# The entry of a one-core decoder kernel: token block on ScalarE's queue, weights first on SyncE's, eight warm-up products from a narrower tile of zeros

## The chip, the cores and the metric

The kernel runs on one core of a Trainium2 chip. Its time is the device's time of one execution in microseconds. The engines are TensorE (PE; its weight loads are listed as PEld), VectorE (DVE), ScalarE (ACT), GpSimd (POOL) and SyncE (SP). SP and ACT issue DMAs on a queue each; "SPq" and "ACTq" in the trace are these issues.

## The reference, cut to what matters

Two transformer layers on 256 tokens of width 1024 in float32. Only the first steps are touched by the change:

```
def reference(x, norm_gain, sb_w_qkv, ...):
    h = x
    for layer in range(DEPTH):                       # DEPTH = 2
        hn = rms_norm(h, norm_gain[layer, 0])
        if layer < N_A_LAYERS:                       # layer 0
            h = h + stick_breaking_attention(hn, sb_w_qkv[layer], sb_w_o[layer])
        else:                                        # layer 1
            h = h + nsa_attention(hn, nsa_w_q[j], nsa_gate_b[j], nsa_w_o[j], shared)
        h = h + sqrelu_mlp(rms_norm(h, norm_gain[layer, 1]), mlp_w1[layer], mlp_w2[layer])
        if layer == N_A_LAYERS - 1:
            shared = nsa_shared_kv(h, kv_norm, nsa_w_kv, cmp_pos, cmp_w1, cmp_w2)
    return rms_norm(h, final_norm)

def stick_breaking_attention(h, w_qkv, w_o):
    qkv = (h @ w_qkv).reshape(b, s, 3, SB_HEADS, HEAD_DIM)
    ...
```

The first product that the kernel computes is the V part of `h @ w_qkv`.

## The kernel before, in words

Every float32 matrix product is done as three products of "float32r" parts: each operand is split into a high part (a cast, on ACT) and a low part (operand less high part, on DVE). For weights the tiles are `raw` (as loaded), `wh` (high, line 180) and `wl` (low, line 186); for tokens the pair `xa` is made from `xin` (the transposed tokens, as loaded) times the norm's gains `gc`. `mm3` issues the three products at lines 261 (high by high), 262 (high tokens by low weights) and 263 (low tokens by high weights).

Layer 0 begins in `layer0`. In the order of the source:

- Nine warm-up products into the bank `warm` (`mm`, line 266). Both operands are `zero`, a tile of 128 x 512 bfloat16 zeros which DVE fills at line 289. Nothing reads their result.
- Buffers for four weight tiles `raw` are taken with `fetch()`. The gains are loaded on ACT's queue (line 672). Then SP's queue gets, in this order: the first of eight token blocks (`x_load(0, 1)`, line 656, 128 x 256 floats, 128 KB), two quarters of the first weight tile (`v_load`, line 124, 256 KB each), the second token block, two more quarters, and so on; behind them constants, the identity and the untransposed tokens (lines 688 to 693).
- `x_cut` makes the high and low parts of a token block: for block 0 the high part on DVE (line 663), for the others on ACT (line 665); the low part always on DVE (line 666).
- `v_proj(k)` for k = 0 to 7 multiplies token block k with its weights: two halves of 512 columns, in each two halves of tokens, in each the three products, into four banks `pv`. So a token block has 12 products, in two groups of six.

ACT begins with loading its table of functions (line 63). In layer 0 the order of PE's work is a planner's, from the order of the source; in much of the rest it is kept as written (`strict`, `keep_in_program_order`). Later weight tiles go through a ring of `raw` buffers, loaded on SP's queue as buffers come free.

Of the kernel before, what the change touches and what calls it, by code (L numbers as in the profile page):

```python
# [9 lines left out]
BF16 = mybir.dt.bfloat16  # L10
# [4 lines left out]
P = 128  # L15
# [37 lines left out]
def hybrid_kernel(ctx, tc, x, xca, xcb, eye, gcols, gfin, wqk, wva, wvb, wo0, wkv, wq, wg, rot, wo1, w1, w2, cw1, cw2, cpos, gate_b, cmask, consts, out):  # L53
    nc = tc.nc

    cp = ctx.enter_context(tc.tile_pool(name="cp", bufs=1))
# [11 lines left out]
    def big(shape, dt, name):  # L68
        return cp.tile(shape, dt, tag="e", name=name, bufs=3)
# [8 lines left out]
    def bank2(name):  # L78
        return ps.tile([P, 512], F32, tag="z", name=name, bufs=4)
# [17 lines left out]
    def fetch():  # L97

        while ahead[0] < len(stream) and stream[ahead[0]][2]:
            ahead[0] += 1  # L100
        if ahead[0] < len(stream):
            j = ahead[0]
            src, n, _ = stream[j]
            if more:
                more[1] += 1
                if more[1] % 5 == 0 and j > more[2]:
                    more.clear()
                    return
            if more and more[1] % 5 == 0:
                raws[j] = more[0]  # L110
            elif j == NV - 1:
                raws[j] = big([P, n], F32, "raw")
            else:
                raws[j] = wp.tile([P, n], F32, tag="raw", name="raw", bufs=4)
            if j in mixed:
                nc.sync.dma_start(raws[j][:, 0:1536], src[:, 512:2048])
            elif j >= NV:
                nc.sync.dma_start(raws[j], src)
            ahead[0] += 1

    def v_load(j, a, b):
        q = 2 * j + a // D
        src = wva[4 * j + a // 512] if q < 3 else wvb[q - 3]
        nc.sync.dma_start(raws[j][:, a:b], src)
# [131 lines left out]
    def pe(ins):  # L256
        if strict[0]:
            tc.keep_in_program_order(ins)
# [6 lines left out]
    def mm(o, a, b, first, last):  # L265
        pe(nc.tensor.matmul(o, a, b, start=first, stop=last, skip_group_check=True))  # L266
# [18 lines left out]
    def cut(hl, a, b):  # L285
        return hl[0][:, a:b], hl[1][:, a:b]

    zero = cp.tile([P, 512], BF16, name="zero")
    nc.vector.memset(zero, 0.0)
    ident = cp.tile([P, P], F32, name="ident")  # L290
    hres = [cp.tile([P, D], F32, name=f"hres{t}") for t in range(T)]
# [46 lines left out]
    def xt_tiles(tag):  # L338
        xp = cp.tile([P, NK, 2, T * P], F32R, tag="x", name=f"x{tag}", bufs=2)
        return xp[:, :, 0, :], xp[:, :, 1, :], xp  # L340
# [292 lines left out]
    def layer0(ap):  # L633

        warm = bank2("warm")
        for i in range(9):
            mm(warm, zero[:, 0:P], zero, True, True)
        xt = xt_tiles("a")
        v = big([P, T, D], F32, "v0")
        pv = [[bank(f"pv{t}{n}") for n in range(2)] for t in range(T)]  # L640
# [11 lines left out]

        xin = big([P, NK, T * P], F32, "xin")

        def x_load(k, m):
            nc.sync.dma_start(xin[:, k:k + m, :].rearrange("p k q -> p (k q)"), xca[k] if m == 1 else xcb)

        def x_cut(k, m):

# [9 lines left out]

        for j in range(NV):  # L670
            fetch()
        nc.scalar.dma_start(gc, gcols)
        x_load(0, 1)
        v_load(0, 0, 512)
        v_load(0, 512, D)
        x_load(1, 1)
        v_load(0, D, D + 512)
        v_load(0, D + 512, 2 * D)
        x_load(2, 1)
        v_load(1, 0, 512)  # L680
        v_load(1, 512, D)
# [520 lines left out]
    def scoped(f, name, *a, bufs=2):  # L1202
        with tc.tile_pool(name=name, bufs=bufs) as ap:
            return f(*a, ap)

    xn = scoped(layer0, "l0")
    nxt = []

# [190 lines left out]
```

## Time and profile before

| | |
|---|---|
| time, median of 3 runs | 600.16 us (599.56 to 601.12) |
| profiled execution, device time | 600.3 us |
| its span, first to last instruction | 598.4 us |
| busy share of the span | PE 98%, PEld 83%, DVE 88%, ACT 70%, POOL 17% |
| granted clock, mean | 0.996 |
| first warm-up product / first product of real data | 1.19 us / 4.65 us |

A row of the timeline reads: start in us, duration in us, engine, line, operation, output <- inputs, shapes, count; in brackets, how long the engine was idle before it and what released it. A row of the waits reads: who waited <- for what: total us, times, longest. In the windows by engine each engine has its busy time and, in brackets, how many instructions; then come the granted clock, the DMA engines' busy share and GB/s. A DMA row has the size of one issue in KB and the median time from issue to landing in us. The ends of products are modelled: a product's row is longer than the distance to the next one.

### The profile page before, as it was taken

How to read it: one execution, taken by the hardware profiler on the slowest of the kernel's cores; microseconds unless marked ns; L12 is line 12 of the kernel's file. 1: busy time of each engine (PE TensorE's matmuls, PEld its weight loads, DVE VectorE, ACT ScalarE, POOL GpSimd, SP SyncE). 2: the span in 40 equal slices, each digit the busy share in tenths (PEclk: the TensorE clock that was granted, in tenths of full speed). 3: DMA queues.
4: the chain of work that ended last, by engine and by line, in shares of the span. 5: the costliest groups of instructions: out<-in, count | busy, mean ns of one | idle time of the engine just before them, and what ended most of it. 6: DMA issues, size and time to landing. Idle time of an engine off the chain costs nothing.

```text
span 598.4 us, 9128 instructions
## 1 busy us (share of the span) xinstructions
PE 587.8 (98%) x3407; PEld 494.0 (83%) x3407; DVE 527.3 (88%) x809; ACT 419.5 (70%) x663; POOL 103.4 (17%) x132
## 2 busy tenths in 40 slices
PE   9999999999999999999999999999999999999994
PEld 6888887888888888888998778678888888888884
DVE  5598997889999999999786898855899999999995
ACT  6677774787777777784841697854887677778753
POOL 0201130020211121000222255460101121111001
PEclk9999999999999999999999999999999999999998
DMA  8977356676999899954477732447678898999501
GB/s 313 423 291 247 141 153 165 245 186 222 264 236 268 271 263 272 287 210 150 156 263 281 251 139 72 142 115 158 173 223 272 214 281 267 246 308 260 175 0 72
DMA packets 27069, 129.81 MB, mean 217 GB/s; under 512 B 3344, under 2 KB 4624, under 8 KB 18320
## 3 DMA queue, kind: packets, MB, share of 16 engines
q1 hardware_dynamic: 19392, 104.18, 47.9%
q0 software_dynamic: 6624, 24.12, 20.4%
q10 hardware_dynamic: 1008, 0.92, 0.5%
q8 instruction: 27, 0.44, 0.3%
q14 instruction: 18, 0.15, 0.1%
HBM read 127.11 MB, written 1.05 MB: 214 GB/s over the span
## 4 chain that ended last, share of the span: by engine, by line
PE 92%; DVE 4%; ACT 2%; issue 1%; POOLq 0%; POOL 0%; DVEq 0%; ACTq 0%
PE pu L266 29%; PE acc L261 8%; PE qk L266 7%; PE acc L262 7%; PE acc L263 7%; PE po L266 3%; PE pu L261 3%; PE pu L262 3%; PE pu L263 3%; PE z L266 2%; PE pk L261 2%; PE pk L262 2%; PE pk L263 2%; PE ptp L269 2%; PE pv L261 1%; PE pv L262 1%
## 5 line engine op out<-in xcount | busy, mean ns | idle before, releaser
L180 ACT CAST wh<-raw 128x1024 fp32r<-128x1024 f32 (+1 forms) x126 | 126.1, 1022 | 35.1 <-PE pq L262 7.7
L266 PE MATMUL pu<-xn,wh 128*128 128x512 f32 x512 | 131.4, 391 | 0.0
L186 DVE TENSOR_TENSOR wl<-raw,wh 128x1024 fp32r<-128x1024 f32 (+1 forms) x90 | 107.1, 1208 | 26.4 <-ACT wh L180 24.5
L266 PEld LDWEIGHTS pu<-xn,wh 128*128 128x128 f32 x512 | 95.3, 188 | 19.4
L266 PE MATMUL pu<-xn,wl 128*128 128x256 f32 x512 | 76.5, 282 | 0.0
L266 PEld LDWEIGHTS pu<-xn,wl 128*128 128x128 f32 x512 | 72.1, 190 | 5.1
L449 ACT COPY mr<-pu 128x512 f32<-128x512 f32 x64 | 37.3, 582 | 36.5 <-PE pu L266 36.1
L388 POOL DMA_DIRECT2D tx<-in_w x26 | 23.0, 930 | 171.4 <-DMA tx<-in_w 170.9
L477 ACT CAST hh<-hx 128x896 fp32r<-128x896 f32 (+1 forms) x32 | 29.6, 925 | 16.7 <-DVE hx L467 11.7
L512 DVE TENSOR_TENSOR wl<-raw,wh 128x2048 fp32r<-128x2048 f32 x18 | 41.1, 2285 | 0.0
L261 PE MATMUL acc<-wh,hh 128*128 128x512 f32 x96 | 37.8, 394 | 0.1
L262 PE MATMUL acc<-wl,hh 128*128 128x512 f32 x96 | 37.6, 392 | 0.0
L136 DVE TENSOR_TENSOR wl<-raw,wh 128x1536 fp32r<-128x1536 f32 x21 | 36.8, 1751 | 0.6 <-ACT wh L135 0.6
L263 PE MATMUL acc<-wh,hl 128*128 128x512 f32 x96 | 37.0, 390 | 0.0
L135 ACT CAST wh<-raw 128x1536 fp32r<-128x1536 f32 x21 | 31.1, 1483 | 5.5 <-PE pu L266 4.7
L387 POOL DMA_DIRECT2D tx<-in_w x20 | 18.7, 936 | 94.2 <-DVE xn L335 57.5
L478 DVE TENSOR_TENSOR hl<-hx,hh 128x896 fp32r<-128x896 f32 (+1 forms) x32 | 34.1, 1066 | 0.3 <-ACT hh L477 0.3
L136 DVE TENSOR_TENSOR tp<-tx,tp 128x1024 fp32r<-128x1024 f32 x28 | 34.1, 1218 | 0.3
L1127 POOL TENSOR_TENSOR pe<-pe,rs 128x512 f32<-128x512 f32 (+1 forms) x32 | 29.3, 946 | 27.0 <-DVE rs L1122 9.9
L266 PE MATMUL qk<-xa,wh 128*128 128x512 f32 x128 | 32.5, 394 | 0.0
L135 ACT CAST tp<-tx 128x1024 fp32r<-128x1024 f32 x28 | 29.5, 1053 | 3.6 <-DVE tx L203 3.5
L1113 ACT ACTIVATE pe<-pe,nm 128x256 f32<-128x256 f32 (+1 forms) x64 | 28.2, 442 | 4.1 <-DVE nm L1111 3.1
(258 smaller groups left out, 1415.0 us busy)
## 6 DMA issues: line engine op xcount, KB each, us to landing
raw<-in_w SPq DMA_DIRECT2D x31, 1024.0 KB, 6.7
tx<-in_w POOLq DMA_DIRECT2D x46, 512.0 KB, 8.6
raw<-in_w SPq DMA_DIRECT2D x21, 768.0 KB, 6.4
raw<-in_wqk SPq DMA_DIRECT2D x8, 1024.0 KB, 8.1
raw<-in_wo SPq DMA_DIRECT2D x8, 1024.0 KB, 4.8
tx<-in_w SPq DMA_DIRECT2D x7, 1024.0 KB, 5.6
raw<-in_wkv SPq DMA_DIRECT2D x6, 1024.0 KB, 4.7
raw<-in_wq SPq DMA_DIRECT2D x4, 1024.0 KB, 4.9
```

The costliest lines, as they stand in the source:

```text
L135: act(nc.scalar.copy(dh[:, r], src[:, r]))
L136: return lambda: dve(nc.vector.tensor_sub(dl[:, r], src[:, r], f32(dh[:, r])))
L180: ins = nc.scalar.copy(h[:, r], raws[j][:, r])
L186: dve(nc.vector.tensor_sub(lo[:, r], raws[j][:, r], f32(h[:, r])))
L261: pe(nc.tensor.matmul(o, a[0], b[0], start=first, stop=False, skip_group_check=True))
L262: pe(nc.tensor.matmul(o, a[0], b[1], start=False, stop=False, skip_group_check=True))
L263: pe(nc.tensor.matmul(o, a[1], b[0], start=False, stop=last, skip_group_check=True))
L266: pe(nc.tensor.matmul(o, a, b, start=first, stop=last, skip_group_check=True))
L449: act(nc.scalar.copy(r[:, f, :], pu))
L477: act(nc.scalar.copy(hh[:, r], hx[:, r]))
L478: dve(nc.vector.tensor_sub(hl[:, r], hx[:, r], f32(hh[:, r])))
L512: dve(nc.vector.tensor_sub(made[i][1], raws[i], f32(made[i][0])))
```

## The change

The tile of zeros keeps its size, but only its first 128 columns are filled and read: the moving operand of a warm-up product is now those 128 columns read four times (a broadcast with step 0). There are eight such products instead of nine. The first token block is issued on ACT's queue ahead of the gains; thus the first two weight quarters stand at the head of SP's queue.

```
-    zero = cp.tile([P, 512], BF16, name="zero")
+    zero = cp.tile([P, 512], BF16, name="zero")[:, 0:P]
     nc.vector.memset(zero, 0.0)
...
         warm = bank2("warm")
-        for i in range(9):
-            mm(warm, zero[:, 0:P], zero, True, True)
+        for i in range(8):
+            mm(warm.rearrange("p (a q) -> p a q", a=4), zero, zero[:, None, :].to_broadcast([P, 4, P]), True, True)
...
-        def x_load(k, m):
-            nc.sync.dma_start(xin[:, k:k + m, :].rearrange("p k q -> p (k q)"), xca[k] if m == 1 else xcb)
+        def x_load(k, m, eng=nc.sync):
+            eng.dma_start(xin[:, k:k + m, :].rearrange("p k q -> p (k q)"), xca[k] if m == 1 else xcb)
...
         for j in range(NV):
             fetch()
+        x_load(0, 1, nc.scalar)
         nc.scalar.dma_start(gc, gcols)
-        x_load(0, 1)
         v_load(0, 0, 512)
         v_load(0, 512, D)
         x_load(1, 1)
```

## The prediction

> **What bounds the kernel now.** I read the page first, for who is busy and which engine the end hangs on.
>
> ```profile
> span 598.4 us, 9128 instructions
> PE 587.8 (98%) x3407; PEld 494.0 (83%) x3407; DVE 527.3 (88%) x809; ACT 419.5 (70%) x663; POOL 103.4 (17%) x132
> PE 92%; DVE 4%; ACT 2%; issue 1%; POOLq 0%; POOL 0%; DVEq 0%; ACTq 0%
> ```
>
> TensorE (PE) is busy in 98% of the span and is 92% of the chain that ended last. The second view is the list of waits, for PE alone:
>
> ```profile
> PE warm L266 <- DVE zero L289: 1.2, 1, 1.2
> PE pss L266 <- DVE kcb L1030: 1.1, 1, 1.1
> PE z L266 <- ACT qu L985: 0.5, 1, 0.5
> PE z L266 <- DVE qkT L746: 0.2, 1, 0.2
> ```
>
> PE waits for 3.0 us in all, and never for a DMA. The three later waits are for DVE and ACT results that are themselves computed from earlier products. So a time gained or lost by PE at the entry has nothing behind it that would swallow it, and moves the end by about as much. The question is only what PE gains before about 8 us. For that I read the chain of waits up to there (start, duration):
>
> ```profile
> 0.86 0.28 DVE zero L289
> 1.19 4.02 PE warm L266 x9
> 5.21 0.85 PE pv L261 x2
> 6.07 0.72 PE pv L262 x2
> 6.79 0.47 PE pv L263 x2
> 7.25 0.23 PE pv L261
> ```
>
> The chain is zero tile, nine warm-up products, first real products (pv). Steps on it: two products in 0.85 us (0.427 each), then two in 0.72, then 0.23 each. Products run at about half pace until some time near 6.5 us, in the second of the two L262 products, and at full pace after. I call that moment the release. The window of the trace over 4 to 5 us gives a granted clock of 1.00 nevertheless, so that column doesn't show the slow stretch; the pace does:
>
> ```profile
> 4.00:5.00 1.00, 1.00 (x4) 0.44 (x2) 0.37 (x1) 0.75 (x2) 0.00 (x0) 1.00 1.07 391
> ```
>
> Next the timeline of the entry by engine (start, duration, engine, line, what; in brackets the idle time before it and its releaser):
>
> ```profile
> 0.74 0.39 SPq L656 DMA_DIRECT2D xin<-in_xca  x1
> 0.74 1.28 ACT L63 ACT_TABLE_LOAD   x1 [0.74 <-PEq L1389]
> 0.77 0.40 ACTq L672 DMA_DIRECT2D gc<-in_gcols  x1
> 0.86 0.27 DVE L289 MEMSET zero<- 128x256 uint32 x1 [0.86 <-PEq L1389]
> 1.19 0.89 SPq L124 DMA_DIRECT2D raw<-in_wva  x2
> 3.20 0.35 DVE L663 TENSOR_SCALAR xa<-xin,gc 128x256 fp32r<-128x256 f32 x1 [2.06 <-DMA gc<-in_gcols]
> 3.98 0.62 ACT L180 CAST wh<-raw 128x512 fp32r<-128x512 f32 x1 [1.97 <-DMA raw<-in_wva]
> 4.65 0.69 PEld L261 LDWEIGHTS pv<-wh,xa 128*128 128x128 f32 x2 [0.34 <-ACT wh L180]
> 4.65 1.42 PE L261 MATMUL pv<-wh,xa 128*128 128x512 f32 x2
> ```
>
> Two things come due almost together. The weights' first block is issued at 1.19, behind the token block on SyncE's queue; its cast runs 3.98 to 4.60, and the load for the first real product starts at 4.65, after 0.34 us idle for that cast. The ninth warm-up product ends at 1.19 + 4.02 = 5.21, and the chain goes through it: the first real product ends about 5.21 + 0.427 = 5.64. The token side (xa) is done at 3.55, a microsecond early.
>
> **The change part by part.**
>
> *Narrower zero tile.* The memset writes a quarter: 64 words instead of 256. In proportion it takes 0.07 us instead of 0.27. A nearest row for a very small DVE instruction is the 128x1 one of 0.15:
>
> ```profile
> 21.50 0.15 DVE L310 TENSOR_SCALAR v<-ss 128x1 f32<-128x1 f32 x1 [1.57 <-ACT sq L306]
> L266 PE MATMUL warm<-zero x9: 609/634/634, 1.2 to 4.6; 128*128 128x512 bf16 x9
> ```
>
> So the first warm-up product starts 0.12 to 0.20 us earlier; I take 0.15, at about 1.04. The moving operand of a warm-up product becomes four readings of the same 128 columns. It still streams 512 columns; no row shows a repeated moving operand in this place. I take the same 0.427 us a product; a repeat that cost a tenth would add 8 x 0.04 = 0.3 us, one that saved a tenth would take off as much, and neither decides alone, since the weights come due at nearly the same time (next).
>
> *One warm-up product fewer.* The spacing is (4.6 - 1.2) / 8 = 0.427 us from first to last start in the row above. The end of the warm-up moves from 5.21 to 5.21 - 0.43 - 0.15 = 4.63. If warm-up alone bound the entry, the first real product would be 0.58 us earlier.
>
> *Weights' first block first on SyncE's queue.* It is issued at 0.74 instead of 1.19, 0.45 us earlier, and every later issue of that queue up to its first wait moves as much. When it lands is bounded from both sides. Upper end: it lands 0.45 earlier. Lower end: nothing is gained, since the token block goes out at the same time on the other queue and both share the engines. Windows of the DMA in the stretch (last two columns: DMA share, GB/s):
>
> ```profile
> 1.50:2.00 0.50, 0.50 (x2) 0.15 (x1) 0.00 (x0) 0.50 (x1) 0.15 (x4) 1.00 0.31 74
> 2.00:2.50 0.50, 0.50 (x3) 0.20 (x2) 0.00 (x0) 0.02 (x1) 0.00 (x0) 1.00 1.07 272
> 2.50:3.00 0.50, 0.50 (x3) 0.23 (x2) 0.00 (x0) 0.00 (x0) 0.00 (x0) 1.00 0.86 203
> 3.00:3.50 0.50, 0.50 (x3) 0.18 (x2) 0.30 (x1) 0.00 (x0) 0.00 (x0) 1.00 0.78 299
> xin<-in_xca SPq DMA_DIRECT2D x4, 128.0 KB, 3.7
> raw<-in_wva SPq DMA_DIRECT2D x6, 256.0 KB, 3.9
> gc<-in_gcols ACTq DMA_DIRECT2D x1, 24.0 KB, 2.3
> ```
>
> From 2.0 us on the engines are 0.78 to 1.07 busy; only 1.5 to 2.0 is slack (0.31). Token block and first weight block are 128 + 256 KB = 393,000 bytes; at the mean of the three rows after 2.0, (272 + 203 + 299) / 3 = 258 GB/s, they take 1.52 us. Started together at about 1.75, they are through at 3.27. The same bytes behind one another ended with the cast's start at 3.98, with perhaps 0.4 us from last byte to the cast (an estimate: the cumulated bytes of the rows reach block, token and gains at about 3.5). So the cast would start at about 3.7: 0.28 earlier. I take 0.3, and 0 and 0.45 as ends.
>
> *Token block and norm weights on ScalarE's queue.* ACT now issues two DMAs at 0.40 each; they lie beside its table load (0.74 to 2.02), and its first compute is at 3.98, so this costs nothing. The gains (gc) go out 0.43 later; gc released xa at 3.20, so xa starts at 3.63 and ends at 3.98, if nothing else delays it. The load for the first product can start at about 4.65 - 0.3 = 4.35: still 0.37 of slack. It would be late only if gc queues behind the token block for over 0.37 us more.
>
> *Next late.* Behind the first product PE must not overtake the following casts. The tightest in the first blocks is the fourth:
>
> ```profile
> 7.58 0.62 ACT L180 CAST wh<-raw 128x512 fp32r<-128x512 f32 x1 [1.11 <-DMA raw<-in_wva]
> 8.23 0.69 DVE L186 TENSOR_TENSOR wl<-raw,wh 128x512 fp32r<-128x512 f32 x1 [0.91 <-ACT wh L180]
> ```
>
> Its parts are there at 8.20 and 8.92. PE reaches it after three blocks of six products: the first ends at 7.25, two more at 12 x 0.227 = 2.72, so at 9.97. A microsecond of slack, with the DMAs that feed it issued 0.45 earlier too. Nothing is late there.
>
> *The sum.* Warm-up allows 0.58, weights 0.3, xa about 0.67: the weights bind, and the first real product starts 0.3 us earlier. But before the release a product takes 0.427 instead of 0.227, so an earlier start within the slow stretch is worth 0.227 / 0.427 = 0.53 of itself, if the release stays where it is: 0.16 us. If the release moves 0.15 earlier with the first warm-up product, another 0.15 x 0.47 = 0.07. The sum is -0.2 us (between 0 and, if the whole 0.45 came through, -0.45). The profiled execution was 600.3 us by the device's count, with a span of 598.4, that is 1.9 outside the span; it would become 600.1. The median of the three runs before, 600.16, is 0.14 below the profiled one, so I predict 599.9 for the median.
>
> **The rivals.**
>
> *Nothing gained at the first product* (no change): the two blocks share the engines wholly and the weights land at 3.98 as before, or gc comes late behind the token block. For it: the shares of 0.78 to 1.07 above. Against it: the slack before 2.0. Time: 600.1 to 600.4. The Trainium skill (DMA: Bandwidth & Descriptors, Issuing engines are not separate DMA queues) says that DMAs started by several engines run on the same 16 DMA engines and interleave, so that a second issuer saves only the issuing time. By that rule the gain at the weights is below the 0.45 of issue, and the sum lies between 0 and -0.2; the shares above agree.
>
> *The release comes late* (slower): the eighth product now ends at 4.63, and the first real product may start with a gap; if the weights gain nothing, its load starts at 4.65 and takes some 0.34, so PE stands idle up to 0.4 us just before the release, where before it was unbroken from 1.19. If that gap resets whatever grants full pace, and the whole run-up has to be done again, the row of the chain prices it: from 1.19 to about 6.5 is 5.3 us at half pace, so up to 5.3 x 0.47 = 2.5 us: 602.6. A reset by half is +1.2: 601.3. It decides where the gap is long enough to count; nothing in this trace has such a gap in the slow stretch. The Trainium skill (TensorE: Matmul & The Clock Gate, Part 1) has the clock gated by a free-running activity window of 3413 ns. By that rule a missed window costs 3.41 x 0.47 = 1.6 us, 601.7, and the release falls differently from run to run whatever the kernel does; one trace can't show that, though the three runs spread over 599.56 to 601.12, which is as wide.
>
> *The release comes early too*: it lies 5.3 us after the first warm-up product now. If the earlier start brings it to 4.6, the slow stretch loses 1.9 us at 0.47, 0.9 us, with the 0.2 of the forecast 599.0. Against it: the start moves only 0.15.
>
> *The order elsewhere moves*: outside the hand-written parts the order on PE is a planner's (the trace shows both token halves' L261 products ahead of L262, where the source has them in turn). If its view of the entry changes the order of later work, the time may move 2 us either way, 598 to 602. Nothing in the trace speaks for it.
>
> **How the numbers follow.** Forecast 0.52; nothing gained 0.23; release late 0.12; release early 0.08; order moved 0.05. A measurement tells about 0.3%, 1.8 us, from no change. Only the late release at over three quarters of its price, or a moved order, goes beyond it upward (0.06); only a moved order, or an early release with luck in the runs, downward (0.04). The range takes the early release (599.0) as its lower end and the late release at most of a half price (601.1) as its upper end, which also takes in the spread of the runs.
>
> **What would show it.** Right: the memset under 0.15 us; warm-up x8 ending near 4.6; xin issued by ACT's queue at 0.77 and gc at about 1.2; the first cast at 3.5 to 3.9; xa done by 4.1; the first real load at 4.2 to 4.5, still waiting for ACT's cast; pace of 0.227 from about 6.4; every later landmark of PE 0.1 to 0.4 us earlier. Wrong: the first load waits for DVE's xa (gc late); the cast still at 3.98 (shared bytes); products at 0.427 beyond 7 us (release late); other changes in the order of PE's groups.

## The result and the profile after

The changed kernel takes 603.33 us (median of 6 runs, 603.06 to 604.61), the kernel before 600.43 (6 runs, 599.56 to 601.12): ratio 1.0053, 95% interval 1.0043 to 1.0063. That is 2.9 us slower, where 0.2 us faster was forecast.

The page after, the rows that answer to the first ones of before:

```profile
span 601.1 us, 9126 instructions
PE 588.8 (98%) x3406; PEld 494.3 (82%) x3406; DVE 527.3 (88%) x809; ACT 420.1 (70%) x663; POOL 103.4 (17%) x132
PE 89%; DVE 5%; ACT 3%; issue 2%; DMA 1%; POOLq 0%; POOL 0%; DVEq 0%; SPq 0%; ACTq 0%
```

PE's busy time is about the same; its share of the chain fell by 3 points, to DVE, ACT, a DMA and "issue". The share says where to look, not how much: the chain can switch between engines that end close together. The waits of PE after (who <- for what: total, times, longest) have two new rows:

```profile
PE pv L261 <- DVE xa L663: 1.7, 1, 1.7
PE pu L263 <- DVE hl L478: 0.2, 1, 0.2
```

The chain of waits after, through the entry (start, duration):

```profile
1.18 3.34 DMA raw<-in_wva
...
4.54 0.63 ACT wh L180
5.17 0.02 issue
5.19 0.03 DVE wl L186
5.22 0.58 issue
5.80 0.36 DVE xa L663
6.16 0.14 issue
6.29 0.77 PE pv L261
7.06 0.43 PE pv L262
...
8.34 0.85 PE pv L263 x2
9.20 0.43 PE pv L261
9.62 0.36 PE pv L262
9.98 0.23 PE pv L263
```

Read against the chain of before, two things stand out. The first real product starts at 6.29 and not at 4.65, and it hangs on xa, which hangs on wl of the second weight block. And products go at 0.43 us until about 9.8; before it was until about 6.5. The timeline shows what the change itself did:

```profile
0.74 0.85 SPq L124 DMA_DIRECT2D raw<-in_wva  x2
0.77 0.39 ACTq L656 DMA_DIRECT2D xin<-in_xca  x1
0.82 0.11 DVE L289 MEMSET zero<- 128x64 uint32 x1 [0.82 <-PEq L1389]
0.99 3.59 PE L266 MATMUL warm<-zero 128*128 128x512 bf16 x8 [0.99 <-DVE zero L289]
1.19 0.45 ACTq L673 DMA_DIRECT2D gc<-in_gcols  x1
3.72 0.62 ACT L180 CAST wh<-raw 128x512 fp32r<-128x512 f32 x1 [1.70 <-DMA raw<-in_wva]
4.37 1.51 DVE L186 TENSOR_TENSOR wl<-raw,wh 128x512 fp32r<-128x512 f32 x2 [3.43 <-ACT wh L180]
5.80 0.35 DVE L663 TENSOR_SCALAR xa<-xin,gc 128x256 fp32r<-128x256 f32 x1
6.29 0.77 PE L261 MATMUL pv<-wh,xa 128*128 128x512 f32 x1 [1.71 <-DVE xa L663]
DMA to landing us min/median/max: 3.5/3.5/3.5
```

The memset, the warm-up's end (0.99 + 3.59 = 4.58) and the first cast (3.72) are where the prediction had them. But DVE now runs two wl before xa. DVE works in order, the second wl waits for ACT's second cast, and xa stands behind it until 5.80. In the program's order on DVE the two kernels differ at this very place: xa, wl, xa, wl before; wl, wl, xa after. The last row above is the landing of gc, issued at 1.19: at 4.7, against 3.1 before (0.77 + 2.3). On DVE's timeline of before, behind the xa at 3.20 come (L666 makes the low part of the token block):

```profile
4.63 0.69 DVE L186 TENSOR_TENSOR wl<-raw,wh 128x512 fp32r<-128x512 f32 x1 [1.08 <-ACT wh L180]
5.24 0.48 DVE L666 SCALAR_TENSOR_TENSOR xa<-xin,gc,xa 128x256 fp32r<-128x256 f32 x1
5.64 0.68 DVE L186 TENSOR_TENSOR wl<-raw,wh 128x512 fp32r<-128x512 f32 x1
```

Everything that DVE and ACT do behind this place, and all that PE does behind the V products, stands in the same order in both traces.

How much of it is in by the end of the V products can be read from the rows of the last of them. The first row is of before, the second of after (min/median/max of the duration, first and last start):

```profile
L263 PE MATMUL pv<-wh,xa x32: 388/389/395, 6.6 to 27.3; 128*128 128x512 f32 x32
```

```profile
L263 PE MATMUL pv<-wh,xa x32: 388/389/632, 8.1 to 29.5; 128*128 128x512 f32 x32
```

To two decimals the last starts are 27.26 and 29.54. So 2.3 of the 2.7 us by which the two spans differ arose before 30 us; the other 0.4 came behind the V products. From first start to last the 96 products take 22.6 us before (from 4.65) and 23.2 after (from 6.29); 95 steps at 0.227 would be 21.6. So the later start is 1.64 us and the longer slow pace another 0.6, over the 1.0 that the kernel before paid too. (A part of that 1.0 is that the row of its first product begins while the ninth warm-up product still runs.) Had the changed kernel run at full pace from its first product on, it would not have paid the 1.0 either; e11 below shows such an execution.

### The profile page after: what moved, and what is told of

Same layout as the page of the kernel before. It is cut to its first block, busy times and chain, and to the rows that moved or that the text cites. A ratio compares the mean times of both kernels' runs of the same rounds, so it can differ in the third digit from the quotient of the medians.

```text
span 601.1 us, 9126 instructions
## 1 busy us (share of the span) xinstructions
PE 588.8 (98%) x3406; PEld 494.3 (82%) x3406; DVE 527.3 (88%) x809; ACT 420.1 (70%) x663; POOL 103.4 (17%) x132
## 4 chain that ended last, share of the span: by engine, by line
PE 89%; DVE 5%; ACT 3%; issue 2%; DMA 1%; POOLq 0%; POOL 0%; DVEq 0%; SPq 0%; ACTq 0%
PE pu L266 28%; PE qk L266 7%; PE acc L261 7%; PE acc L262 7%; PE acc L263 7%; PE po L266 3%; PE pu L263 3%; PE pu L261 3%; PE pu L262 3%; PE z L266 2%; PE pk L261 2%; PE pk L263 2%; PE pk L262 2%; PE ptp L269 2%; PE pv L261 1%
## 5 line engine op out<-in xcount | busy, mean ns | idle before, releaser
L261 PE MATMUL acc<-wh,hh 128*128 128x512 f32 x96 | 37.8, 394 | 0.1
```

The lines of the kernel that those rows point to most:

```text
L261: pe(nc.tensor.matmul(o, a[0], b[0], start=first, stop=False, skip_group_check=True))
```

## The experiments

Theories: A, DVE's new order puts xa behind two wl. B, gc lands late behind the token block. C, eight warm-up products are too few. After the first four, R: besides the waiting, an idle stretch of PE makes the release of full pace late; against W: waiting is all. Ratios are to the kernel before, run beside, with 95% intervals.

**e1, the warm-up part alone**: narrow tile, eight products, all DMAs as before.

```
+    zero = cp.tile([P, 512], BF16, name="zero")[:, 0:P]
...
+        for i in range(8):
+            mm(warm.rearrange("p (a q) -> p a q", a=4), zero, zero[:, None, :].to_broadcast([P, 4, P]), True, True)
```

> The kernel before with the warm-up part of the change alone: narrower zero tile, eight products; all DMAs as before. On DVE the planner keeps the order of before (xa, wl, xa, wl). Theory A (the loss comes from DVE: xa is put behind two wl in DVE's order, so that the first real product waits for 1.7 us, and the slow pace lasts longer): nothing of that is here, the first real load still starts at 4.65 on ACT's cast, 600.0 to 600.9 us, ratio 0.9995 to 1.001. Theory B (gc lands late behind the token block on ACT's queue, whatever DVE's order): also 600.0 to 600.9. Theory C (too few warm-up products: PE stands idle before the first real product and the release comes late): a gap from about 4.6 to 5.0 and a release after 7 us, 601.3 to 603 us.

600.22 us (599.76 to 601.91), before 600.25: 1.0002 [0.9994, 1.0011]. No change. PE stood idle for 0.5 us and the profiled execution was nevertheless at full pace from its first real product on. C in its plain form falls; one of eleven runs was at 601.91, the others at 600.6 or less.

**e2, the DMA part alone**, with the nine products of before.

```
+        x_load(0, 1, nc.scalar)
         nc.scalar.dma_start(gc, gcols)
-        x_load(0, 1)
```

> The kernel before with the DMA part of the change alone: token block on ACT's queue ahead of gc, weights first on SP's queue; nine warm-up products of the full tile. The planner gives DVE the same order as in the changed kernel: two wl ahead of xa. Theory A: xa again at about 5.8, first real product at about 6.3, 602.5 to 603.5 us, ratio 1.0035 to 1.005; the ninth warm-up product shortens the idle time of PE from 1.7 to about 1.1 us. Theory B: about the same, 601 to 603.5. Theory C (warm-up decides): 600.0 to 600.8.

601.52 us: 1.0025 [1.0016, 1.0034]. The loss is here, and DVE's order has turned with it; but the median was lower than either A or the changed kernel would have it. The eleven runs form two groups: seven at 601.26 to 601.61, three at 603.13 to 603.45, one between. The profiled execution, 603.13, has the slow pace up to 9.7. If the waiting is the same in all runs (one alone has a trace), it makes some 1.2 us, and something that comes and goes makes 1.9.

**e3, DVE's order alone**, in the kernel before with its queues and its nine products:

```
+        pinned[0] = True
+        W(i_v[0], 1024)
         x_cut(0, 1)
+        pinned[0] = False
         v_proj(0)
```

`W(i_v[0], 1024)` makes both weight splits first. The high part of the first token block goes through `dve(...)` too, so that it is kept in the order of the source.

> The kernel before, queues and warm-up untouched, with DVE's order alone changed to that of the changed kernel (two wl, then xa), by emitting the first two weight splits ahead of the token cut and keeping that order. Theory A: xa waits for the second wl, which waits for the second cast (done at 5.47): wl to 6.4, xa to 6.75, first real product at about 6.8, 603 to 604.5 us, ratio 1.0045 to 1.007, though all DMAs land as before. Theory B (late gc): gc lands early here, 600.2 to 600.9. Theory C: 600.2 to 600.9.

603.35 us (601.6 to 604.64): 1.0049 [1.0036, 1.0061]. The order alone costs as much as the whole change, with every DMA issued as before (in the profiled execution, 604.64, the slowest of the six, the second weight block landed 0.8 later than in that of before, so xa is later still than expected). In the timeline of its profile:

```profile
6.31 0.69 DVE L186 TENSOR_TENSOR wl<-raw,wh 128x512 fp32r<-128x512 f32 x1 [1.17 <-ACT wh L180]
6.92 0.35 DVE L663 TENSOR_SCALAR xa<-xin,gc 128x256 fp32r<-128x256 f32 x1
7.41 0.77 PE L261 MATMUL pv<-wh,xa 128*128 128x512 f32 x1 [2.20 <-DVE xa L663]
```

DVE stands idle for 1.17 us ahead of the second wl, with gc landed at 3.2: it keeps to its order. The slow pace lasts to 13 us.

**e4, the changed kernel with DVE's order put back**: xa first. (Its low part comes ahead of the two wl too, and PE takes four L261 products first, where in the kernel before it takes two.)

```
+        pinned[0] = True
         x_cut(0, 1)
         v_proj(0)
+        pinned[0] = False
```

> The changed kernel with DVE's order alone put back: the high part of the first token block is kept ahead of the weights' low parts. Queues and eight warm-up products as changed. Theory A alone: the first real product waits for what comes later of the cast (4.34) and gc: 599.8 to 600.6 us, ratio 0.999 to 1.000. Theory A with B (gc landed at 1.19 + 3.5 = 4.69 in the changed kernel, against 3.2 before): xa 4.69 to 5.05, first real load at about 5.1, 0.45 later than before, with PE idle from 4.6 to 5.1: 600.8 to 601.8 us, ratio 1.0005 to 1.002. Theory C: 602.5 to 603.5, as the changed kernel.

602.42 us (one run 600.35, five 602.17 to 602.6): 1.003 [1.0018, 1.0041]. Higher than A with B expected, and only 0.1 below the range of C. The first real product starts at 5.29 and waits for gc; its chain:

```profile
1.19 3.49 DMA gc<-in_gcols
...
4.79 0.36 DVE xa L663
5.15 0.14 issue
5.29 2.05 PE pv L261 x4
```

So B is real: it is what holds the first product when A is undone. The slow pace remains as well, in the profiled execution to 9.7, and one run of the six lies 2 us below the others.

**e5, twelve warm-up products in the changed kernel**, nothing else.

```
-        for i in range(8):
+        for i in range(12):
```

> The changed kernel with twelve warm-up products instead of eight, nothing else. They reach to 0.99 + 12 x 0.427 = 6.1 us, just ahead of the first real product, which still waits for xa until about 6.3. Theory R (of the 2.9 us some 1.9 are a late release: the idle stretch of PE from 4.4 to 6.3 makes the slow pace last until 9.6, and only the rest is waiting): the first real product is at full pace, 601.1 to 601.7 us, ratio 1.0012 to 1.0022, and no run above 602.5. Theory W (the loss is the waiting for xa alone): 603.0 to 603.6, as the changed kernel.

601.77 us (601.61 to 602.58 and one of 604.16): 1.0032 [1.002, 1.0044]. Nothing else than zeros was added, and 1.3 to 1.6 us came back against the changed kernel (+1.55 instead of +2.9 over the kernel before beside each; 603.33 - 601.77 directly). The first real product starts no earlier, but it and all that follow are at full pace:

```profile
0.99 5.30 PE L266 MATMUL warm<-zero 128*128 128x512 bf16 x12 [0.99 <-DVE zero L289]
6.34 0.47 PE L261 MATMUL pv<-wh,xa 128*128 128x512 f32 x1
6.65 0.39 PE L262 MATMUL pv<-wl,xa 128*128 128x512 f32 x1
```

W falls. The median is 0.1 above R's range, and two runs, 602.58 and 604.16, are above its limit of 602.5; 604.16 is the profiled execution, and it has one wait of 2.4 us elsewhere, which no other kernel's profile shows:

```profile
PE pu L266 <- ACT mr L449: 2.4, 1, 2.4
```

**e6, order put back as in e4, and `range(10)` for the warm-up.**

> The changed kernel with DVE's order put back (xa ahead of the weights' low parts), as before, and ten warm-up products, which reach to 5.26 us, where xa lets the first real product start. With eight it had runs near 602.4 and one at 600.35. Theory R: the ones near 602.4 go, 600.3 to 600.9 us, ratio 1.000 to 1.001; what is left over the kernel before is the late gc. Theory W: 602.2 to 602.6, as with eight.

601.21 us (600.68 to 602.21): 1.0015 [1.0006, 1.0024]. The group near 602.4 is gone but for 602.21, as R has it; the level is 0.3 above its range. In the profiled execution (601.48) the third weight block came late too:

```profile
7.89 1.27 ACT L180 CAST wh<-raw 128x512 fp32r<-128x512 f32 x2 [2.07 <-DMA raw<-in_wva]
```

a wait that R hadn't counted.

**e7, gc first on ACT's queue, order kept as in e4 (and for the second token block), nine narrow products.**

```
+        nc.scalar.dma_start(gc, gcols)
         x_load(0, 1, nc.scalar)
-        nc.scalar.dma_start(gc, gcols)
```

> A version meant to do what the change describes: weights first on SP's queue, on ACT's queue gc ahead of the token block, DVE's order kept (xa, then the weights' low parts), narrow zeros, nine warm-up products (to 4.83). gc should land near 3.1 as before; the token block is issued at 1.19 and has 128 KB to move beside the weights: landed at 3.6 to 4.4, xa ready at 4.0 to 4.8, first real load 4.2 to 4.9. Theory R with gc as the cause of the lateness: 599.6 to 600.4 us, ratio 0.999 to 1.0003. If the token block is as late here as gc was: first load at 5.1, 600.5 to 602.

600.61 us (600.43 to 601.41): 1.0009 [1.0000, 1.0017]. The best of the versions with weights first, and no better than before. It is 0.2 above R's range and inside the other one: now the token block is the late one, and the first real product starts at 5.25.

```profile
3.54 0.62 ACT L180 CAST wh<-raw 128x512 fp32r<-128x512 f32 x1 [1.53 <-DMA raw<-in_wva]
4.75 0.35 DVE L663 TENSOR_SCALAR xa<-xin,gc 128x256 fp32r<-128x256 f32 x1 [3.82 <-DMA xin<-in_xca]
```

The cast came 0.4 earlier than before, xa 1.55 later. What the weights gain on their queue the token side loses.

**e8, e9 and e10: seven, five and ten narrow warm-up products in the kernel before** (e1 with `range(7)`, `range(5)`, `range(10)`), all else untouched. These ask R alone: no operand is issued later.

> The kernel before, DMAs and DVE's order untouched, with seven narrow warm-up products: they end at 4.0, and PE stands idle until the first real load at 4.65 to 5.1, which waits for ACT's cast as before. Theory R: the idle stretch of about 1 us makes the release late in many runs, which then lie near 602, others near 600.2; median 600.5 to 602.2, highest above 601.8. Theory W: nothing waits longer than before, 600.0 to 600.5, no run above 601.5.

> The kernel before with five narrow warm-up products, all else as before: they end at 3.1 us, 1.5 to 2 us ahead of the first real load, which waits for ACT's cast as before. Theory R (an idle stretch of PE ahead of the release puts the release off): with seven, half of the runs were near 600.1 and half near 601.6; with five nearly all are late, median 601.5 to 602.3. Theory W (only waiting for operands costs time): 600.0 to 600.5, since the operands come as before.

> The kernel before with ten narrow warm-up products, all else as before: they reach to 5.26 us, past the first real load's operands (4.65), so PE has no idle stretch. Theory R: no late run, all within 599.6 to 600.9, highest below 601.2, median 600.0 to 600.5. Theory W: the first real product is held up by 0.3 us of zeros, 600.3 to 600.8, with the same scatter as the kernel before.

| products | median us | runs above 601.1 | ratio |
|---|---|---|---|
| 5 | 601.31 (600.81 to 603.59) | 6 of 8 | 1.0028 [1.0016, 1.0039] |
| 7 | 600.80 (599.76 to 602.43) | 6 of 12 | 1.0010 [1.0000, 1.0019] |
| 8 (e1) | 600.22 (599.76 to 601.91) | 1 of 11 | 1.0002 [0.9994, 1.0011] |
| 9, full tile (before, beside e5 to e8) | 600.22 (599.54 to 601.22) | 3 of 30 | 1 |
| 10 | 599.98 (599.51 to 602.08) | 1 of 11 | 1.0002 [0.9994, 1.0011] |

Beside the other experiments 1 of 43 runs of the kernel before was above 601.1. The shorter the warm-up ahead of the gap, the more runs are late. With ten one run was at 602.08, against R's expectation of none; with five the median fell short of R's by 0.2. In five's profiled execution the second cast was late as well, so not all of its loss is pace. With seven the profiled execution was the fastest one, 599.76; that its late runs are late by pace is inferred from their times.

**e11, the changed kernel with gc ahead of the token block**, DVE's order as changed.

> The changed kernel with the two issues on ACT's queue swapped: gc first, then the token block. DVE's order stays that of the changed kernel (two wl ahead of xa). Theory A (DVE's order sets when xa is made, not gc's landing): xa still starts at about 5.8, behind the second wl, 603.0 to 603.6 us, as the changed kernel. Theory B (gc's lateness sets it): gc lands near 3.5, and the time falls to 601 to 602.

603.64 us (601.39 to 605.27): 1.0063 [1.005, 1.0076]. A holds: gc early (landed at 3.8) and DVE's order unchanged brings nothing. The profiled execution was the fastest of the six, 601.39, and it is the plainest view of the two prices apart; the last two rows are the last of the V products and the landing of gc:

```profile
5.71 0.35 DVE L663 TENSOR_SCALAR xa<-xin,gc 128x256 fp32r<-128x256 f32 x1
6.20 0.47 PE L261 MATMUL pv<-wh,xa 128*128 128x512 f32 x1 [1.62 <-ACT xa L665]
6.51 0.40 PE L262 MATMUL pv<-wl,xa 128*128 128x512 f32 x1
L263 PE MATMUL pv<-wh,xa x32: 388/389/397, 7.2 to 27.9; 128*128 128x512 f32 x32
DMA to landing us min/median/max: 3.0/3.0/3.0
```

(The profile puts the wait down to L665, the second token block's high part, which ends together with the xa of L663.) The same wait as in the changed kernel (first product at 6.20 instead of 6.29), but full pace from there: 601.39 instead of 603.06. The V products end 0.6 later than before here (27.88 against 27.26), and 2.3 later in the changed kernel.

**When full pace is granted, in all thirteen traces.** Each trace also records from when the full clock was granted. The views show 1.00 ahead of the first record too, which is why their clock column hides the slow stretch. The first record falls on the end of the slow pace each time. From there the full clock lasted 587.09 us in eight traces and 590.51 in five, 3.41 apart, which are 172 and 173 times 3.4133: so in these traces the clock changes on a grid of 3.413 us, and where the grid lies against the program differs from execution to execution. The table gives PE's busy share in the grid's last stretch of 3.413 us ahead of the release, and the highest in any such stretch before that.

| profile | full clock from (us) | last stretch | highest earlier |
|---|---|---|---|
| before | 6.50 | 1.00 | 0.55 |
| after | 9.77 | 1.00 | 0.57 |
| e1 | 5.07 | 0.86 | 0.20 |
| e2 | 9.74 | 1.00 | 0.70 |
| e3 | 12.95 | 1.00 | 0.73 |
| e4 | 9.72 | 1.00 | 0.80 |
| e5 | 6.34 | 0.99 | 0.57 |
| e6 | 3.94 | 0.86 | 0.00 |
| e7 | 6.42 | 0.93 | 0.59 |
| e8 | 3.83 | 0.83 | 0.00 |
| e9 | 9.66 | 0.88 | 0.54 |
| e10 | 6.21 | 1.00 | 0.53 |
| e11 | 5.00 | 0.88 | 0.17 |

A stretch at 0.83 or more was followed by the full clock, one at 0.80 or less never. So an idle stretch of PE costs a further 3.413 us of slow pace, 1.6 us of time (an estimate: 3.413 x 0.2 / 0.427), if it takes a stretch of the grid below that share, and nothing if the stretch keeps its share or full pace is granted already: in the changed kernel's trace the stretch from 2.94 to 6.35 was half idle, in e11's the one from 1.58 to 5.00 was nearly full. Where between 0.80 and 0.83 the limit lies, no run shows; the shares rest on modelled ends of products.

## Why the prediction was wrong, point by point

- *What bounds the kernel, and that a loss at the entry stays*: right. The 2.3 us of the V products are found again at the end (2.7). The other 0.4 belong to the DMA part and not to the late start: from the last start of a V product to the span's end it is 571.2 to 571.3 us in before, e1, e3, e8, e9 and e10, and 571.6 to 571.7 in after, e2, e4, e6, e7 and e11 (e5 has its wait of 2.4 besides). In e7's profile they are 0.4 of a loss of 0.6. One piece, 0.2, is the new wait for hl; it is in the profiles of the changed kernel and of every version with the DMA part, and in none of the others. Why, no run shows; it isn't the order of the instructions.
- *Narrower zeros*: taken 0.15 earlier, measured 0.20 (0.99 against 1.19). The spacing stayed at (3.59 - 0.61) / 7 = 0.426, a product's own row being 0.61, so four readings of 128 columns cost what 512 columns do. Right.
- *One product fewer*: end at 4.63 predicted, 4.58 measured, and worth nothing by itself (e1).
- *Weights first*: 0.28 worked out, 0.3 taken, 0.26 measured (3.98 to 3.72). Over all profiles the cast starts at 3.79 to 4.42 with the queues of before (mean 4.0) and at 3.53 to 3.96 with the DMA part (mean 3.7). Right; and without use, since the weights were no longer what came last.
- *Token block and gains on ACT's queue*: **here a step failed.** xa was put at 3.63 to 3.98, gc being only issued 0.43 later, "if nothing else delays it". gc landed 3.5 us after its issue instead of 2.3: it stands behind 128 KB on its own queue, which share the engines with the weights. The condition was named (over 0.37 of queueing), but the sum put it at nothing, and the rival that names it (gc comes late) priced it at no more than the lost gain; it was 1.2 us. The row for it was there: the DMA engines busy at 0.78 to 1.07 from 2.0 us on. I used it for the weights and not for gc. In e7 and e11, where gc is first on its queue but the weights are moved beside it, it took 2.9 and 3.0: so about half of the 1.2 comes with the weights and half from standing behind the token block. In the changed kernel this step is covered by the next one: gc was there at 4.7, DVE came to xa at 5.80. The Trainium skill (DMA: Bandwidth & Descriptors, Issuing engines are not separate DMA queues) has DMAs of several issuers run on the same 16 DMA engines and interleave. e7 agrees: a second issuer moved the lateness from one operand to the other.
- *The order elsewhere moves*: **the step that cost most.** It was given 0.05, with "Nothing in the trace speaks for it", and sought in PE's later work. It happened on DVE, at the first instruction behind the memset, where an order of two wl ahead of xa turns a token block that is ready into one that waits for the second cast: xa ran at 5.80 and not at 3.63, so the first real product waited for xa and not for the weights, and started at 6.29 and not at about 4.35. e3 and e11 show that the order alone is enough; e1 and e2, that the DMA part turned it. I asked what a later xa would delay, and not what the planner does with an operand that moves behind another in its own plan.
- *The release comes late* (0.12): the mechanism was right in its second form, a missed window, and had the wrong trigger. I had it depend on a gap of 0.4 us; the gap was 1.7, made by xa. (In e1's profile a gap of 0.5 did nothing.) A whole run-up done again, the first form, didn't show: the release came 3.5 us after the first real product and not 5.3. Its price was put at 2.5, or 1.6 by the Trainium skill's window (TensorE: Matmul & The Clock Gate, Part 1). Measured, changed kernel against e5: 1.3 to 1.6. The groups of e2 and e4 are some 2 us apart. The rule's free-running window agrees with the traces: the grid of 3.413 us against the page's 3413 ns, and its place against the program differs between executions. So the times of one kernel fall into groups (e2; e4, e8 and e11 by their times too).
- *The sum*: -0.2 had only the weights as the binding side. What came was a first product 1.64 us later, and the slow pace on top. That warm-up, memset and cast came out as forecast changed nothing, since none of them bound the entry any more.

So of the 2.7 us between the two profiled spans, 0.6 are the later first product (by e11, in which full pace comes in time), 1.7 the late release on top of it, and 0.4 arise behind the V products. The medians are near it: e2's lower group lies 1.2 above the kernel before, against 1.0 for the first and the last together, and e5 gives 1.3 to 1.6 for the release. How the 0.6 would split between gc and DVE's order can't be told by taking one away: with the order undone gc is the one waited for (e4), with gc early the order is (e11). No version here beat the kernel before by an amount that can be measured; e1 and e10 came closest, at ratio 1.0002 each.

## What to carry to other kernels

When an operand's load is moved, look up every instruction on its in-order consumer that could now be planned ahead of it: the order of issue is part of the change even if no line of it is edited. Price a small load that is put behind a large one by the bytes ahead of it on its own queue and beside it on the others: here gc took 2.3, 3.0 and 3.5 us from issue to landing. And keep warm-up products running up to the first real one, while full pace isn't granted yet: here the gap cost more by pace (1.3 to 1.6 us) than by the wait that made it (0.6 of the later first product).

## What was not expected of the hardware

The pace after an idle stretch isn't one price but two outcomes. With the same instructions in the same order on PE, DVE and ACT, and two issues on ACT's queue swapped, the first real product after 1.6 to 1.7 us of idle PE was once at full pace (e11, 601.39 us) and once at half pace for 3.5 us more (the changed kernel's profile, 603.06). What decided was where the grid of 3.413 us lay: the release came at 5.00, during the idle stretch itself, in the one and at 9.77 in the other. In e6 and e8 it came as early as 3.9, some 2.9 us after the first warm-up product. The mean granted clock of the profile, 0.996 to 0.997 in both, doesn't tell the two apart; the spacing of the products, 0.43 or 0.23 us, does.
